# A block kernel's last product: from eight and eight to ten and ten feature tiles in seven half-size products

## The chip, the cores and the metric

The kernel runs on one core of one Trainium2 chip. The metric is the device time of one execution in microseconds (us). The core has five engines that run side by side, each with its own instruction queue in order: TensorE (PE, matmuls; PEld is its loading of the stationary operand), VectorE (DVE), ScalarE (ACT), GpSimd (POOL) and SyncE (SP). SP and POOL here mostly issue transfers, which 16 DMA engines carry out. A transfer that adds to what lies at its destination is issued by POOL; plain ones go out from SP.

## The reference, cut to what matters

The program is one layer of an encoder on 512 tokens (T) of width 1024 (D): a first feed-forward half-step, a mixer, a second feed-forward half-step (FFN2) and a final norm. The change touches the end of FFN2 and the final norm:

```python
D_FF = 2816
x = x + 0.5 * swiglu(rms_norm(x, ffn2_norm), ffn2_w1, ffn2_w3, ffn2_w2)
out = rms_norm(x, final_norm)

def swiglu(h, w1, w3, w2):
    return (jax.nn.silu(h @ w1) * (h @ w3)) @ w2
```

The last product is `H @ w2`, with `H` of 512 tokens by 2816 features and `w2` of 2816 by 1024. In tiles of 128 that is four token tiles, 22 feature tiles and two column halves of 512. All is float32; each operand is cut into a high part (`hi`, in a reduced format of TensorE) and the rest (`lo`), and three matmuls (hi hi, lo hi, hi lo) make one product.

## The kernel before, in words

**Seven products for eight.** `ByTokens.run` makes the last product with tokens as rows. Of the 22 feature tiles, the first `KS` = 8 (half 1) and the next 8 (half 2) go through the scheme in which a product of two matrices, each cut into two by two blocks, takes seven block products and some sums instead of eight products. The blocks of `H` are token halves by feature halves, those of `w2` feature halves by column halves. The products are called M1 to M7. The remaining 6 feature tiles (`plain`, from `KP` = 16 on) are multiplied in the plain way, first for two banks ("F"), later for the two others ("L").

**Units.** Work is cut into units of two feature tiles. Each unit of a product is 12 matmuls of 128 rows by 512 columns. `order` lists the units: M1, M2, F, M5, M6, M3, M7, L for column half 1, M4, L for column half 0. The loop at the end runs over `n`: `product(n)` issues the matmuls of unit n, then the steps of `plan[n]` are issued, then `ready(n + 3)` prepares the unit three ahead. The last three units are multiplied by `final`, first for token tile 2, then for the two halves of token tile 3. Nearly every instruction is issued under `keep`, so that each engine executes in the order that the code gives.

**Preparation.** `prep` casts a weight tile of 128 x 1024 to its high part on ScalarE (line 1979) and makes the rest on VectorE (line 1905), in one of three pairs of buffers; so a cast waits until TensorE is done with the unit three back. For M6, M3 and M7 `parts` also cuts a sum of blocks of `H` (`S2`, `S4`, `S3`).

**Sums of H.** For each unit u, `wa` and `wb` put the high and low parts of the two halves together (`R[u]`), `s1` to `s4` make the four sums, and `cast` and `rest` write the cut first sum over the second half of the tokens of `h` (units of M5 read it from there).

**Sums of w2.** They are made by transfers: `chain[u]` is loaded with block 11, and adding transfers from POOL (`onto`, line 1896) then put further blocks on it, each when `ready` is done with the state before: block 12 after M1, block 22 after M5, block 21 after M3 (for M4). `b21` and `b22` hold blocks 21 and 22; after M3, block 12 is added onto `b22` (for M7). Plain loads go through `fetch` (line 1892) from SP.

**Results.** Banks X, Y, Z, W hold the sums on TensorE's side. `first_snap`, `fifth_snap` and `sixth_snap` (line 2007) scale what stands in X, Z and X again into SBUF tiles `x0`, `m5` and `up`. `c11`, `c22`, `c12` add or subtract banks (line 1908). `residual` adds the layer's input from a DRAM copy (`xtok`) by transfers from POOL. `square_of`, `measure`, `finish` and `others` do the final norm for token tiles 0 and 1 and prepare that of 2 and 3: squares with their sum on ScalarE (line 2100), the root by a logarithm and an exponential (lines 2108, 2109), scaling and storing.

Of the kernel before, what the change touches and what calls it, by code (L numbers as in the profile page):

```python
# [13 lines left out]
ALU = mybir.AluOpType  # L14
# [7 lines left out]
KD = D // P  # L22
DFF = 2816
KF = DFF // P
KS = 8
DA = 512
NP = DA // P
C = 32
# [24 lines left out]
def kernel(  # L53
# [335 lines left out]
    def f32(ap):  # L389
        return ap.bitcast(F32)  # L390
# [1461 lines left out]
    class ByTokens:  # L1852
# [27 lines left out]
        def run(s, hh, hl, h, w2, hp):  # L1880
# [3 lines left out]
            def part(k0, c):  # L1884
                return w2[0][k0 * P:(k0 + 2) * P, c * T:(c + 1) * T].rearrange("(k p) c -> p k c", p=P)
# [4 lines left out]
            def fetch(tag, k0, c):  # L1890
                to = unit(tag)
                keep(nc.sync.dma_start(to, part(k0, c)))
                return to

            def onto(to, src):
                keep(nc.gpsimd.dma_start(to, src, accum_op=ALU.add))
# [7 lines left out]
            def two(to, a, b, op=ALU.subtract):  # L1904
                keep(dve.tensor_tensor(to, a, b, op=op))

            def three(to, ps, f, b, op=ALU.add):
                keep(dve.scalar_tensor_tensor(to, ps, f, b, op0=ALU.mult, op1=op))

            chain = [t[:] for t in s.sv.first_raw]  # L1910
            for u in (2, 3):
                chain.append(wp.tile([P, 2, T], F32, tag="raw", name="raw", bufs=4)[:])
                keep(nc.sync.dma_start(chain[u], part(2 * u, 0)))
            X, Y = [bank(f"tx{a}", pr) for a in range(2)], [bank("ty0", pr), bank("ty1")]
            Z, W = [bank("tz0"), bank("tz1", pf)], [bank(f"tw{a}", pf) for a in range(2)]
            bank_of = [[Y[0], Z[0]], [Y[1], Z[1]], [X[0], W[0]], [X[1], W[1]]]

            def single(tag, name):
                return xp.tile([P, 2, H], F32, name=name, tag=tag)[:]

            S2, S4 = [fp.tile([P, 8, H], F32, name=f"s{i}", tag=f"O{i}") for i in range(2)]
            S2, S4 = [[S[:, 2 * u:2 * u + 2] for u in range(NU)] for S in (S2, S4)]
            S3 = [xp.tile([P, 2, H], F32, name="s3", tag="acc", bufs=2)[:] for _ in range(2)]
            S3 += [fp.tile([P, 2, H], F32, name="s3", tag="sq7")[:], single("rstd", "s3")]
            R = [None] * NU

            def wa(u):
# [4 lines left out]
            def wb(u):  # L1932
                for k in range(2):
                    kk = KS + 2 * u + k
                    to = R[u][1][k]
                    two(over(to, hh[kk]), f32(hh[kk]), f32(hl[kk]), ALU.add)

            def s1(u):
                v = R[u][1][2][:, :, H:T]
                two(v, R[u][0][2][:, :, H:T], v)  # L1940

            def cast(u):
                keep(act.copy(h[:, 2 * u:2 * u + 2, 0, H:T], R[u][1][2][:, :, H:T]))

            def rest(u):
                hi, lo = [h[:, 2 * u:2 * u + 2, i, H:T] for i in range(2)]
                two(lo, R[u][1][2][:, :, H:T], f32(hi))

            def s2(u):
                two(S2[u], R[u][1][2][:, :, H:T], R[u][0][2][:, :, 0:H])  # L1950

            def s3(u):
                two(S3[u], R[u][0][2][:, :, 0:H], R[u][0][2][:, :, H:T])

            def s4(u):
                two(S4[u], R[u][1][2][:, :, 0:H], S2[u], ALU.add)
# [17 lines left out]
            def prep(src):  # L1974
                if len(wide) % 3 == 2:
                    hi, lo = fp.tile([P, 2, T], F32R, name="whi", tag="fg")[:], unit("E30", F32R, "wlo")
                else:
                    hi, lo = [wp.tile([P, 2, T], F32R, tag=t, name=t, bufs=2)[:] for t in ("whi", "wlo")]
                keep(act.copy(hi, src))
                two(lo, src, f32(hi))  # L1980
                wide.append((hi, lo))

            def seventh(n, banks, left, start=False):
# [25 lines left out]
                return got  # L2009

            K2, KP = KS, 2 * KS
            b21 = [fetch(t, K2 + 2 * u, 0) for u, t in enumerate(("E10", "E11", "E20", "E21"))]
            plain = range(KP, KF, 2)

            def all_of(m):
                return [(m, u) for u in range(NU)]

            order = all_of("M1") + all_of("M2") + [(("F", k0), c) for k0 in plain for c in range(2)]
            order += all_of("M5") + all_of("M6") + all_of("M3") + all_of("M7") + [(("L", k0), 1) for k0 in plain]
            order += all_of("M4") + [(("L", k0), 0) for k0 in plain]  # L2020
            made = {}

            def source(m, u):
                if m in ("M1", "M5", "M6", "M4"):
# [7 lines left out]
            def ready(n):  # L2032
                m, u = order[n]
                if m in ("M6", "M3", "M7"):
                    made["left", m, u] = parts({"M6": S2, "M3": S4, "M7": S3}[m][u])
                if n > 1:
                    prep(source(m, u))
                if m == "M1":
                    onto(chain[u], part(2 * u, 1))
                if m == "M5":  # L2040
                    onto(chain[u], part(K2 + 2 * u, 1))
                if m == "M3":
                    onto(made["b22", u], part(2 * u, 1))
                    if u == NU - 1:
                        for v in range(NU):
                            onto(chain[v], part(K2 + 2 * v, 0))

            def product(n):
                m, u = order[n]
# [27 lines left out]
                made["m5"] = snap(Z, "m5", 2)  # L2077

            def sixth_snap():
                made["up"] = snap(X, "up", 0)  # L2080

            def c11():
                for a in range(2):
# [5 lines left out]

            def c12():  # L2090
                for a in range(2):
                    three(made["up"][a], Z[a][:], sc[:, a:a + 1], made["up"][a], ALU.subtract)

            def residual(name, t0, c):
                for a in range(2):
# [7 lines left out]
            def biased(t, q):  # L2103
                keep(dve.tensor_scalar(sc[:, 16 + t:17 + t], q, 1.0 / D, RMS_EPS, op0=ALU.mult, op1=ALU.add))
# [4 lines left out]
                keep(act.activation(r, r, AF.Exp, scale=-0.5))  # L2109

            def gains():
                made["fg"] = hp.tile([P, D], F32, name="fgain", tag="E01")[:]
# [5 lines left out]

            def square_of(name, t):
                biased(t, square(made[name][t], t, 0))  # L2120

            def measure(t):
                root(t, square(made["up"][t], t, 1))
# [2 lines left out]
                keep(nc.sync.dma_start(out[0, t * P:(t + 1) * P, c * T:(c + 1) * T], src))  # L2126

            def finish(t):
                for c, src in ((0, made["x0"][t]), (1, made["up"][t])):
                    three(src, src, sc[:, 20 + t:21 + t], made["fg"][:, c * T:(c + 1) * T], ALU.mult)  # L2130
                    store(t, c, src)

            def others():
                for a in range(2):
# [9 lines left out]
                3: [lambda: rest(0), lambda: wa(1), lambda: load("F", 16, 0, "E10")],  # L2144
                4: [lambda: wb(1), lambda: load("F", 16, 1, "E11")],
                5: [first_snap, lambda: s1(1), lambda: s2(1), lambda: load("F", 18, 0, "E20")],
                6: [lambda: cast(1), lambda: s3(1), lambda: s4(1), lambda: load("F", 18, 1, "E21")],
                7: [lambda: rest(1), lambda: wa(2)],
                8: [lambda: wb(2), lambda: load("F", 20, 0, "E10")],
                9: [lambda: s1(2), lambda: s2(2), lambda: load("F", 20, 1, "E11")],  # L2150
                10: [lambda: cast(2), lambda: s3(2), lambda: s4(2)],
                11: [lambda: rest(2), lambda: wa(3), lambda: b22(0, "E20")],
                12: [lambda: wb(3), lambda: b22(1, "E21")],
                13: [lambda: s1(3)],
                14: [lambda: cast(3), lambda: s2(3)],
                15: [lambda: rest(3), lambda: s4(3)],
                16: [lambda: s3(3)],
                17: [fifth_snap],
                18: [lambda: b22(2, "E00"), lambda: b22(3, "E01")],
                21: [sixth_snap, lambda: load("L", 16, 1, "E10")],  # L2160
                22: [c11, lambda: load("L", 18, 1, "E11")],
                24: [lambda: c22(W, sc), lambda: residual("x0", 0, 0)],
                25: [lambda: load("L", 20, 1, "E20")],
                27: [act_set, lambda: load("L", 16, 0, "E21")],
                28: [lambda: load("L", 18, 0, "E00"), gains],
                29: [lambda: load("L", 20, 0, "E10")],
                30: [lambda: c22(X, neg)],
                31: [lambda: residual("m5", 2, 1), kept],
                33: [c12, lambda: residual("up", 0, 1)],
                34: [lambda: square_of("x0", 0), lambda: square_of("x0", 1)],  # L2170
                36: [others],
            }
            for n in range(-1, len(order) - 3):
                if n >= 0:
# [84 lines left out]
```

## Time and profile before

| | |
|---|---|
| median of 3 runs | 1118.36 us (1118.07 to 1118.51) |
| the profiled execution's own time | 1118.83 us |
| its span, first to last instruction | 1117.1 us |
| granted TensorE clock | 0.999 |
| TensorE busy | 99% of the span |
| the last product, first to last matmul | 1002.12 to 1111.19 us |

The span is that of the program's instructions in one profiled execution; what lies around it, 1.73 us, belongs to the measured time. In rows of the timeline a number in brackets is the time that the engine stood idle before the instruction, followed by what ended it. A group's mean duration can be longer than the step from one start to the next, since an engine begins an instruction before the one ahead of it has wholly ended.

### The profile page before, as it was taken

The page shows a single profiled execution, that of the slowest core. Times are in us where ns is not written, and L with a number is a line of the kernel's source. Part 1 is how long each engine was busy: PE and PEld are TensorE (multiplying, and loading weights), DVE is VectorE, ACT ScalarE, POOL GpSimd, SP SyncE. Part 2 cuts the span into 40 slices and gives each one's busy share as a digit, 9 for nine tenths or more (in the row PEclk, how much of TensorE's full clock was granted, in tenths as well). Part 3 has the DMA queues.
Part 4 walks back from the last instruction along what each step waited for, and adds up shares of the span by engine and source line. Part 5 has one row for each costly group of instructions (what it writes and reads, how often), then busy time and mean ns, then how long its engine had stood idle before and what let it go on. Part 6 is the DMA issues. An engine that isn't in the chain of part 4 may idle for free.

```text
span 1117.1 us, 19566 instructions
## 1 busy us (share of the span) xinstructions
PE 1109.1 (99%) x7658; PEld 975.8 (87%) x7658; DVE 910.8 (82%) x1427; ACT 651.2 (58%) x1088; POOL 110.9 (10%) x175
## 2 busy tenths in 40 slices
PE   9999999999999999999999999999999999999997
PEld 7899999998887888888777787788999999998886
DVE  6889999989556788768777677878889999989876
ACT  6646555644335855454779768534766655655564
POOL 2000000010000112321000001113000000001240
PEclk9999999999999999999999999999999999999999
DMA  8433333353344343345322226543344433358696
GB/s 265 128 94 105 114 96 112 96 180 110 116 123 119 83 118 102 113 121 140 78 58 74 86 89 199 163 132 95 97 121 123 132 96 114 96 168 226 152 213 184
DMA packets 199322, 140.60 MB, mean 126 GB/s; under 512 B 10654, under 2 KB 178910, under 8 KB 199230
## 3 DMA queue, kind: packets, MB, share of 16 engines
q1 hardware_dynamic: 186094, 110.51, 33.8%
q0 software_dynamic: 10752, 27.79, 10.1%
q8 instruction: 60, 0.98, 0.4%
q10 hardware_dynamic: 2384, 1.05, 0.3%
q14 instruction: 32, 0.26, 0.1%
HBM read 124.45 MB, written 14.88 MB: 125 GB/s over the span
## 4 chain that ended last, share of the span: by engine, by line
PE 97%; DVE 1%; DMA 1%; ACT 0%; issue 0%; SPq 0%; DVEq 0%
PE za L143 23%; PE zc L143 14%; PE pgt L143 8%; PE pd L143 6%; PE pk L143 6%; PE tx L1902 4%; PE ppj L1702 4%; PE pw L143 4%; PE pq L143 4%; PE pb L143 3%; PE pa L143 3%; PE tz L1902 3%; PE pv L143 2%; PE ty L1902 2%; PE pl L143 1%; PE lp L1490 1%
## 5 line engine op out<-in xcount | busy, mean ns | idle before, releaser
L134 ACT CAST whi<-raw 128x1024 fp32r<-128x1024 f32 (+2 forms) x93 | 90.0, 969 | 101.8 <-issue 16.6
L135 DVE TENSOR_TENSOR wlo<-raw,whi 128x1024 fp32r<-128x1024 f32 (+2 forms) x93 | 104.5, 1123 | 21.3 <-ACT whi L134 20.9
L143 PE MATMUL zc<-xh,wlo 128*128 128x256 f32 x296 | 83.7, 283 | 0.0
L143 PE MATMUL zc<-xl,whi 128*128 128x256 f32 x296 | 83.7, 283 | 0.0
L143 PE MATMUL zc<-xh,whi 128*128 128x256 f32 x296 | 83.7, 283 | 0.0
L143 PE MATMUL za<-e,wtwo 128*128 128x256 f32 x480 | 64.2, 283 | 0.0
L143 PEld LDWEIGHTS za<-e,wtwo 128*128 128x128 f32 x480 | 59.6, 188 | 0.0
L512 ACT CAST wtwo<-wsum 128x1024 fp32r<-128x1024 f32 x37 | 38.9, 1051 | 31.4 <-PE za L143 31.4
L143 PEld LDWEIGHTS zc<-xl,whi 128*128 128x128 f32 x296 | 56.7, 191 | 0.0
L143 PEld LDWEIGHTS zc<-xh,wlo 128*128 128x128 f32 x296 | 56.7, 191 | 0.0
L143 PEld LDWEIGHTS zc<-xh,whi 128*128 128x128 f32 x296 | 56.6, 191 | 0.0
L143 PE MATMUL pgt<-xh,whi 128*128 128x512 f32 x128 | 53.0, 414 | 0.0
L515 DVE TENSOR_TENSOR wlo<-raw,whi 128x1024 fp32r<-128x1024 f32 x41 | 50.0, 1219 | 2.5 <-ACT whi L512 2.5
L524 DVE TENSOR_TENSOR wsum<-wsum,raw 128x512 f32<-128x512 f32 x74 | 50.9, 688 | 1.2
L524 DVE TENSOR_TENSOR wsum<-raw 128x512 f32<-128x512 f32 x74 | 50.7, 685 | 0.0
L143 PE MATMUL pgt<-xh,wlo 128*128 128x512 f32 x128 | 50.1, 391 | 0.0
L143 PE MATMUL pgt<-xl,whi 128*128 128x512 f32 x128 | 50.0, 391 | 0.0
L512 ACT CAST whi<-wsum 128x1024 fp32r<-128x1024 f32 x37 | 38.8, 1048 | 16.9 <-PE zc L143 13.0
L512 ACT CAST whi<-raw 128x1024 fp32r<-128x1024 f32 x41 | 43.1, 1051 | 8.9 <-PE zc L143 7.9
L598 ACT ACTIVATE fs<-fa 128x512 f32<-128x512 f32 x39 | 24.7, 632 | 38.5 <-DVE fa L631 31.3
L515 DVE TENSOR_TENSOR wtwo<-wsum,wtwo 128x1024 fp32r<-128x1024 f32 x37 | 45.1, 1218 | 0.0
L515 DVE TENSOR_TENSOR wlo<-wsum,whi 128x1024 fp32r<-128x1024 f32 x37 | 45.1, 1218 | 0.0
(692 smaller groups left out, 3619.2 us busy)
## 6 DMA issues: line engine op xcount, KB each, us to landing
raw<-in_ffn_w_dram SPq DMA_DIRECT2D x106, 512.0 KB
raw<-in_w_in_dram SPq DMA_DIRECT2D x40, 512.0 KB
wu<-in_ffn_w_dram SPq DMA_DIRECT2D x20, 512.0 KB
raw<-in_ffn_w_dram POOLq DMA_DIRECT2D x12, 512.0 KB, 7.6
raw<-in_w_out_dram SPq DMA_DIRECT2D x8, 512.0 KB
raw<-in_ffn_w_dram SPq DMA_DIRECT2D x8, 384.0 KB
gsave<-gs SPq DMA_DIRECT2D x9, 256.0 KB
xin<-in_x_dram SPq DMA_DIRECT2D x4, 512.0 KB
```

The costliest lines, as they stand in the source:

```text
L134: marks["wide"] = act.copy(hi[:], raw[:])
L135: marks["rest"] = (eng or dve).tensor_tensor(lo[:], raw[:], hi[:].bitcast(F32), op=ALU.subtract)
L143: mm = pe.matmul(ps, w, x_, start=first and n == 0, stop=last and n == 2, skip_group_check=chain)
L512: keep(act.copy(dst, src))
L515: keep(dve.tensor_tensor(dst, src, f32(hi), op=ALU.subtract))
L524: keep(dve.tensor_tensor(to, a, b, op=ALU.add))
L598: keep(act.activation(sa[:], a_[:], AF.Silu))
L1490: keep(pe.matmul(av[half(q), j * P:(j + 1) * P], vt[k][:, h * 64:(h + 1) * 64], s.trs[q][:, o:o + P], start=k == 0, stop=k == b))
L1702: keep(pe.matmul(ps[:], a[:, k, :], y[k][b], start=k == 0 and n == 0, stop=k == NP - 1 and n == 2))
L1902: keep(pe.matmul(ps[:], a, b, start=start, stop=stop, skip_group_check=True))
```

## The change

`KS` goes from 8 to 10: 20 of the 22 feature tiles go through the seven products (five units each), and one unit of two feature tiles stays plain. Because there is no room for all weights, three of them (two of `b21` and one of F) are loaded as two half tiles each into tiles `x5`, `x6` and `x7` that held the norm's input (`halved`, `pair`). The sums of H's high and low parts for the fifth unit are made by transfers within SBUF into `x5` and `x6` (`joined`: two copies from SP and two adding transfers from POOL for each half), and its further sums go tile by tile (`each`). M5 and M6 take the units in the order 0, 1, 2, 4, 3. The adding transfers of M4's first two units are issued after M6 instead of after M3; the residuals of `m5` and `up` earlier. `up` is snapped with a negative factor, so that its residual can be added before `c12`, and `c12` adds. `square_of` also multiplies `x0` by the gain; `measure` and `finish` move from behind the loop to steps 34 and 35, and `finish` scales `x0` on ScalarE instead of VectorE.

```diff
-KS = 8
+KS = 10
...
+            chain.append(fetch("E10", 8, 0))
...
+            def pair(n, name):
+                return [xp.tile([P, T], F32, name=f"{name}{i}", tag=f"x{i}{n}")[:] for i in "hl"]
+
+            def halved(n, k0, c):
+                to = pair(n, "wh")
+                for k in range(2):
+                    keep(nc.sync.dma_start(to[k], w2[0][(k0 + k) * P:(k0 + k + 1) * P, c * T:(c + 1) * T]))
+                return to
+
+            def joined(u, n):
+                if R[u] is None:
+                    R[u] = []
+                R[u].append(pair(5 + n, f"r{n}"))
+                ks = [n * KS + 2 * u + k for k in range(2)]
+                for to, kk in zip(R[u][n], ks):
+                    keep(nc.sync.dma_start(over(to, hh[kk]), f32(hh[kk])))
+                for to, kk in zip(R[u][n], ks):
+                    onto(over(to, hh[kk]), f32(hl[kk]))
+
+            def each(u, to, a, b, op=ALU.subtract):
+
+                if len(R[u][0]) == 3:
+                    two(to[2], a[2], b[2], op)
+                else:
+                    for k in range(2):
+                        two(to[k], a[k], b[k], op)
...
-            b21 = [fetch(t, K2 + 2 * u, 0) for u, t in enumerate(("E10", "E11", "E20", "E21"))]
+            b21 = [fetch(t, K2 + 2 * u, 0) for u, t in enumerate(("E11", "E20", "E21"))]
+            b21 += [halved(7, K2 + 6, 0), halved(5, K2 + 8, 0)]
             plain = range(KP, KF, 2)
+            turns = 0, 1, 2, 4, 3
...
-            made = {}
+            made = {(("F", KP), 0): halved(6, KP, 0)}
...
                     onto(made["b22", u], part(2 * u, 1))
-                    if u == NU - 1:
-                        for v in range(NU):
-                            onto(chain[v], part(K2 + 2 * v, 0))
+                if m == "M3" and u == NU - 1 or m == "M6" and u < 2:
+                    for v in range(2, NU) if m == "M3" else (u,):
+                        onto(chain[v], part(K2 + 2 * v, 0))
...
-                made["up"] = snap(X, "up", 0)
+                made["up"] = snap(X, "up", 24)
...
-                    three(made["up"][a], Z[a][:], sc[:, a:a + 1], made["up"][a], ALU.subtract)
+                    three(made["up"][a], Z[a][:], sc[:, a:a + 1], made["up"][a])
...
             def square_of(name, t):
                 biased(t, square(made[name][t], t, 0))
+                two(made[name][t], made[name][t], made["fg"][:, 0:T], ALU.mult)
...
             def finish(t):
-                for c, src in ((0, made["x0"][t]), (1, made["up"][t])):
-                    three(src, src, sc[:, 20 + t:21 + t], made["fg"][:, c * T:(c + 1) * T], ALU.mult)
-                    store(t, c, src)
+                r, x, up = sc[:, 20 + t:21 + t], made["x0"][t], made["up"][t]
+                keep(act.activation(x, x, AF.Copy, scale=r))
+                store(t, 0, x)
+                three(up, up, r, made["fg"][:, T:D], ALU.mult)
+                store(t, 1, up)
...
+                7: [lambda: rest(1), lambda: wa(2), lambda: joined(4, 0)],
+                8: [lambda: wb(2), lambda: joined(4, 1), lambda: b22(0, "E20")],
+                9: [lambda: s1(2), lambda: s2(2), lambda: b22(1, "E21")],
+                10: [lambda: cast(2), lambda: s3(2), lambda: s4(2)],
+                11: [lambda: rest(2), lambda: wa(3)],
+                12: [lambda: s1(4), lambda: wb(3), lambda: b22(2, "E11")],
+                13: [lambda: cast(4), lambda: s1(3), lambda: rest(4)],
+                14: [lambda: cast(3), lambda: s2(3), lambda: rest(3)],
+                15: [lambda: s2(4)],
+                16: [lambda: s4(4)],
+                17: [lambda: s4(3), fifth_snap],
+                18: [lambda: s3(3), lambda: residual("m5", 2, 1)],
+                19: [lambda: s3(4), lambda: b22(3, "E00"), lambda: b22(4, "E01")],
+                21: [sixth_snap],
+                22: [c11],
+                24: [lambda: c22(W, sc), lambda: residual("x0", 0, 0), lambda: residual("up", 0, 1)],
+                25: [lambda: load("L", KP, 1, "E20")],
+                26: [lambda: load("L", KP, 0, "E21")],
+                28: [act_set, gains],
+                31: [lambda: c22(X, neg), kept],
+                33: [c12],
+                34: [lambda: square_of("x0", 0), lambda: square_of("x0", 1), lambda: measure(0), lambda: measure(1)],
+                35: [others, lambda: finish(0), lambda: finish(1)],
...
-            measure(0)
-            measure(1)
-            finish(0)
-            finish(1)
-            ends = list(enumerate(plain, len(order) - 3))
+            ends = list(enumerate((K2 + 6, K2 + 8, KP), len(order) - 3))
```

More of the change, by code (lines that the diff above doesn't have):

```diff
@@ L1921, in run @@
             S2, S4 = [fp.tile([P, 8, H], F32, name=f"s{i}", tag=f"O{i}") for i in range(2)]
-            S2, S4 = [[S[:, 2 * u:2 * u + 2] for u in range(NU)] for S in (S2, S4)]
+            S2, S4 = [[S[:, 2 * u:2 * u + 2] for u in range(4)] + [tmp("s", [P, 2, H])[:]] for S in (S2, S4)]
             S3 = [xp.tile([P, 2, H], F32, name="s3", tag="acc", bufs=2)[:] for _ in range(2)]
-            S3 += [fp.tile([P, 2, H], F32, name="s3", tag="sq7")[:], single("rstd", "s3")]
+            S3 += [fp.tile([P, 2, H], F32, name="s3", tag="sq7")[:], single("rstd", "s3"), tmp("s3", [P, 2, H])[:]]
             R = [None] * NU
@@ L1938, in s1, with rows, whole3 @@
+            def each(u, to, a, b, op=ALU.subtract):
[4 more added lines that the diff above has]
+                        two(to[k], a[k], b[k], op)
+            def rows(ts, c0):
+                return [t[..., c0:c0 + H] for t in ts]
+            def whole3(t):
+                return [t[:, 0], t[:, 1], t]
             def s1(u):
-                v = R[u][1][2][:, :, H:T]
-                two(v, R[u][0][2][:, :, H:T], v)
+                a21, a22 = rows(R[u][0], H), rows(R[u][1], H)
+                each(u, a22, a21, a22)
@@ L1942, in cast @@
             def cast(u):
-                keep(act.copy(h[:, 2 * u:2 * u + 2, 0, H:T], R[u][1][2][:, :, H:T]))
+                to, v = h[:, 2 * u:2 * u + 2, 0, H:T], rows(R[u][1], H)
+                if len(v) == 3:
+                    keep(act.copy(to, v[2]))
+                else:
+                    for k in range(2):
+                        keep(act.copy(to[:, k], v[k]))
             def rest(u):
                 hi, lo = [h[:, 2 * u:2 * u + 2, i, H:T] for i in range(2)]
-                two(lo, R[u][1][2][:, :, H:T], f32(hi))
+                each(u, whole3(lo), rows(R[u][1], H), whole3(f32(hi)))
@@ L1949, in s2 @@
             def s2(u):
-                two(S2[u], R[u][1][2][:, :, H:T], R[u][0][2][:, :, 0:H])
+                each(u, whole3(S2[u]), rows(R[u][1], H), rows(R[u][0], 0))
             def s3(u):
-                two(S3[u], R[u][0][2][:, :, 0:H], R[u][0][2][:, :, H:T])
+                each(u, whole3(S3[u]), rows(R[u][0], 0), rows(R[u][0], H))
             def s4(u):
-                two(S4[u], R[u][1][2][:, :, 0:H], S2[u], ALU.add)
+                each(u, whole3(S4[u]), rows(R[u][1], 0), whole3(S2[u]), ALU.add)
@@ L1978, in prep @@
                     hi, lo = [wp.tile([P, 2, T], F32R, tag=t, name=t, bufs=2)[:] for t in ("whi", "wlo")]
-                keep(act.copy(hi, src))
-                two(lo, src, f32(hi))
+                if type(src) is list:
+                    for k in range(2):
+                        keep(act.copy(hi[:, k], src[k]))
+                    for k in range(2):
+                        two(lo[:, k], src[k], f32(hi[:, k]))
+                else:
+                    keep(act.copy(hi, src))
+                    two(lo, src, f32(hi))
                 wide.append((hi, lo))
@@ L2011, in run, with all_of @@
             K2, KP = KS, 2 * KS
-            b21 = [fetch(t, K2 + 2 * u, 0) for u, t in enumerate(("E10", "E11", "E20", "E21"))]
+            b21 = [fetch(t, K2 + 2 * u, 0) for u, t in enumerate(("E11", "E20", "E21"))]
+            b21 += [halved(7, K2 + 6, 0), halved(5, K2 + 8, 0)]
             plain = range(KP, KF, 2)
-            def all_of(m):
-                return [(m, u) for u in range(NU)]
+            turns = 0, 1, 2, 4, 3
+            def all_of(m, us=range(NU)):
+                return [(m, u) for u in us]
             order = all_of("M1") + all_of("M2") + [(("F", k0), c) for k0 in plain for c in range(2)]
-            order += all_of("M5") + all_of("M6") + all_of("M3") + all_of("M7") + [(("L", k0), 1) for k0 in plain]
+            order += all_of("M5", turns) + all_of("M6", turns) + all_of("M3") + all_of("M7") + [(("L", k0), 1) for k0 in plain]
             order += all_of("M4") + [(("L", k0), 0) for k0 in plain]
-            made = {}
+            made = {(("F", KP), 0): halved(6, KP, 0)}
             def source(m, u):
@@ L2111, in gains @@
             def gains():
-                made["fg"] = hp.tile([P, D], F32, name="fgain", tag="E01")[:]
+                made["fg"] = hp.tile([P, D], F32, name="fgain", tag="E11")[:]
                 keep(nc.sync.dma_start(made["fg"], final_norm.unsqueeze(0).broadcast_to([P, D])))
@@ L2143, in run @@
                 2: [lambda: cast(0), lambda: s3(0), lambda: s4(0)],
[L2144 to L2149, printed above, removed]
@@ L2150, in run @@
-                9: [lambda: s1(2), lambda: s2(2), lambda: load("F", 20, 1, "E11")],
-                10: [lambda: cast(2), lambda: s3(2), lambda: s4(2)],
[L2152 to L2171, printed above, removed]
+                3: [lambda: rest(0), lambda: wa(1), lambda: load("F", KP, 1, "E11")],
+                4: [lambda: wb(1)],
+                5: [first_snap, lambda: s1(1), lambda: s2(1)],
+                6: [lambda: cast(1), lambda: s3(1), lambda: s4(1)],
```

## The prediction

> **What bounds the kernel now.** I read the page first: its span, its busy table and the chain that ended last.
>
> ```profile
> span 1117.1 us, 19566 instructions
> PE 1109.1 (99%) x7658; PEld 975.8 (87%) x7658; DVE 910.8 (82%) x1427; ACT 651.2 (58%) x1088; POOL 110.9 (10%) x175
> PE 97%; DVE 1%; DMA 1%; ACT 0%; issue 0%; SPq 0%; DVEq 0%
> ```
>
> TensorE sets the end. Then I read the chain in order of time over the last product (columns: start, us, what, count).
>
> ```profile
> 1002.12 10.91 PE tx L1902 x48
> 1013.03 13.60 PE ty L1902 x60
> ...
> 1091.91 14.96 PE tx L1902 x66
> 1106.87 2.15 PE tz L1902 x18
> 1109.02 2.17 PE tx L1902 x18
> ...
> 1111.22 0.49 DVE yt L1908
> ...
> 1113.33 0.40 DVEq L2255
> ```
>
> The stage runs from 1002.12 to 1111.19 without a gap. A unit (two feature tiles, twelve 512-wide matmuls) takes 13.60 / 5 = 2.72 us, and 40 units at 2.72 are 108.8 of the 109.07 us. The last three units are cut differently: token tile 2 first, 18 matmuls that end at 1106.87, then tile 3 in two halves, 2.15 + 2.17 us. After the last matmul a tail of 5.9 us goes to the span's end. So what TensorE does less is gained, provided that no weight or left operand comes late. What stands behind TensorE is read from the timelines of VectorE and ScalarE around 1027 to 1042 (start, duration, instruction).
>
> ```profile
> 1026.85 1.22 DVE L1905 TENSOR_TENSOR wlo<-wu,whi 128x1024 fp32r<-128x1024 f32 x1
> ...
> 1036.87 1.22 DVE L1905 TENSOR_TENSOR wlo<-raw,whi 128x1024 fp32r<-128x1024 f32 x1
> 1038.01 1.29 DVE L1905 TENSOR_TENSOR rb<-hh,hl 128x512 f32<-128x512 f32 x2
> ...
> 1040.35 0.68 DVE L1905 TENSOR_TENSOR rb<-ra,rb 128x512 f32<-128x512 f32 x1
> 1040.95 1.22 DVE L1905 TENSOR_TENSOR wlo<-raw,whi 128x1024 fp32r<-128x1024 f32 x1
> ```
> ```profile
> 1036.64 1.06 ACT L1979 CAST whi<-raw 128x1024 fp32r<-128x1024 f32 x1 [1.62 <-PE ty L1902]
> ```
>
> VectorE runs back to back; from start to start a full weight rest costs 1.14 us, a 512-wide add 0.6. ScalarE casts the weight three units ahead, as soon as TensorE releases the buffer.
>
> **The change, part by part.** *Products.* Seven products of 4 units and 12 plain units (40) become seven of 5 and 4 plain (39): one unit of 2.72 us goes. With every other time kept, TensorE would end at 1108.47 and token tile 2 at 1104.15.
>
> *Feature tiles 8, 9, 18, 19.* Their sum of high and low parts is made by eight 256 KB transfers inside SBUF (four copies from SP, four adding ones from POOL) instead of VectorE. They start when the weights that lie in the same tiles have been cut up: the second pair follows the rest of unit 10, 1026.85 + 1.14 = 1028.0 (one step more or less from the halved form is below 0.1). VectorE needs them in `s1(4)`, behind the rest of unit 14, 1036.87 + 1.14 = 1038.0. No transfer of this kind is in the trace. The nearest rows are the transfer rates (stretch, busy of PE, PEld, DVE, ACT, POOL, clock, DMA share, GB/s): weight loads alone, adding transfers alone, both together, stores of 256 KB.
>
> ```profile
> 1052.00:1056.00 4.00, 4.00 (x20) 3.30 (x19) 3.02 (x4) 3.22 (x5) 0.00 (x0) 1.00 1.05 402
> 1042.00:1050.00 8.00, 8.00 (x37) 6.64 (x36) 7.36 (x10) 4.20 (x5) 2.57 (x3) 1.00 1.12 197
> 1078.00:1096.00 18.00, 18.00 (x81) 14.92 (x80) 11.60 (x13) 8.51 (x10) 3.24 (x4) 1.00 1.10 266
> ...
> 1106.00:1108.00 2.00, 2.00 (x15) 1.85 (x14) 2.00 (x4) 0.31 (x1) 0.00 (x0) 1.00 1.01 381
> ```
> ```profile
> wu<-in_ffn_w_dram POOLq DMA_DIRECT2D x4, 512.0 KB, 5.7
> ```
>
> An adding transfer of 0.524 MB moves in 0.524 / 0.197 = 2.7 us, so 3.0 of the 5.7 us to landing are fixed. Low end: copies at 381 GB/s (0.7 each) with 1 us fixed land at 1030.4, and the two adding ones at 1030.4 + 3.0 + 2 x 1.33 = 1036.1. High end: the copies take the 3.0 too and the adding ones share the engines with the loads of `b22` issued just behind (266 / 2 = 133 GB/s, 1.97 each): 1032.4 + 3.0 + 3.9 = 1039.3. I take 1038, nearer the high end since those loads are certain. After it VectorE has `s1(4)` 0.7, `wb(3)` 1.2, a rest 1.14, `s1(3)` 0.7, `rest(4)` 0.7: 4.4 us, so 1042.4, and unit 15 (the fifth product's unit 4) starts at 1002.12 + 15 x 2.72 = 1042.9. Cost 0, with 0.5 us to spare; at the high end 0.8 us. Queued behind `s1(4)` on VectorE are the rests of units 15 to 17, for which TensorE waits two units later.
>
> *VectorE's other work*: the fifth unit's five combinations are 3.3 us against one rest less (1.14) and no `wa`, `wb`; from step 12 to 19 each step has 2.3 to 3.0 us of work in 2.72. Hidden by the two units that weights are ahead; without that cover 1 us.
>
> *Loads and freed tiles.* `chain[4]` and five `b21` go out at once, three in tiles freed with the last slots before 1002; 512 KB at 402 GB/s is 1.3 us. Beside the adding transfers these loads take 3.9 us each at worst, and the last is wanted at unit 7's end, 1023.9; from 1001, six at half rate are in by 1024.6 at the very latest, at full rate by 1009; TensorE wants unit 10 only at 1029.3. Cost 0.
>
> *The queue of adding transfers late in the stage.* Before, POOL issues these (start, us, what):
>
> ```profile
> 1069.13 1.20 POOL L1896 DMA_DIRECT2D wu<-in_ffn_w_dram  x1 [1.72 <-DVE wlo L1905]
> 1069.86 5.34 POOL L1896 DMA_DIRECT2D raw<-in_ffn_w_dram  x4
> 1072.72 4.26 POOL L1896 DMA_DIRECT2D x<-xtok  x2
> 1086.37 1.72 POOL L1896 DMA_DIRECT2D m<-xtok  x2 [9.39 <-PE tz L1902]
> 1094.48 1.73 POOL L1896 DMA_DIRECT2D up<-xtok  x2 [6.39 <-DVE up L1908]
> ```
>
> The landing line of the two `x` transfers says how deep that queue is: they go out from 1072.72 on and land at about 1094.6 and 1096.7, 2.1 us apart, which is the half share of 266.
>
> ```profile
> DMA to landing us min/median/max: 21.9/22.7/23.5
> ```
>
> After the fourth M3 transfer (1069.13 + 5.7 = 1074.8) the changed queue holds one more of M3, three of M4, two `x`, two `up`: 4 x 0.524 + 4 x 0.262 = 3.14 MB. Beside it SP loads two weights, the gains and `yt`, 2.1 MB. Shared: 2 x 2.1 / 0.266 = 15.8 us; the other 1.04 MB alone: 5.3 us. The second `up` lands at about 1074.8 + 21.1 + 0.6 = 1096.5. Bounds: 1094 if the loads take little of it, 1099 if the queue starts one unit later.
>
> *The end.* Here I expect the gain to go. `c12` used to run before its residual was added; now it reads it, so VectorE waits there for `up` (before: 1093.27), with the rests of units 36 to 38 behind it. And `measure` and `finish` stand ahead of the casts of units 37 and 38, where before they followed all casts. Rows of ScalarE and VectorE:
>
> ```profile
> 1093.76 1.06 ACT L1979 CAST whi<-raw 128x1024 fp32r<-128x1024 f32 x1 [1.67 <-PE tx L1902]
> 1094.71 0.63 ACT L2100 ACTIVATE junk<-x 128x512 f32<-128x512 f32 x1
> ...
> 1100.15 0.63 ACT L2100 ACTIVATE junk<-m 128x512 f32<-128x512 f32 x1
> ...
> 1100.78 0.62 ACT L2100 ACTIVATE junk<-m 128x512 f32<-128x512 f32 x1
> ...
> 1102.88 0.62 ACT L2100 ACTIVATE junk<-up 128x512 f32<-128x512 f32 x1
> ...
> 1104.06 0.62 ACT L2100 ACTIVATE junk<-up 128x512 f32<-128x512 f32 x1
> ```
> ```profile
> 1061.80 1.27 ACT L2007 ACTIVATE up<-tx,small 128x512 f32<-128x512 f32 x2 [0.92 <-PE tx L1902]
> ```
> ```profile
> 1092.13 1.23 DVE L1905 TENSOR_TENSOR wlo<-raw,whi 128x1024 fp32r<-128x1024 f32 x1 [1.49 <-ACT whi L1979]
> 1093.27 1.40 DVE L1908 SCALAR_TENSOR_TENSOR up<-tz,small,up 128x512 f32<-128x512 f32 x2
> ...
> 1101.49 0.68 DVE L1905 TENSOR_TENSOR m<-m,fgain 128x512 f32<-128x512 f32 x1
> ...
> 1104.19 0.75 DVE L1908 SCALAR_TENSOR_TENSOR x<-x,small,fgain 128x512 f32<-128x512 f32 x1
> 1104.86 0.74 DVE L1908 SCALAR_TENSOR_TENSOR up<-up,small,fgain 128x512 f32<-128x512 f32 x1
> ...
> 1106.91 1.14 DVE L1908 SCALAR_TENSOR_TENSOR yt<-tx,small,yt 128x512 f32<-128x512 f32 x2
> ```
>
> From start to start: a cast 0.95, a square 0.63, a `measure` 1.18, a ScalarE scaling 0.64, a VectorE 512-wide step 0.6 to 0.7. With `up` landing at L: second `c12` L + 0.1 to L + 0.8; rest 36 to L + 1.9; the small sum that the root waits for, L + 2.1; first root L + 2.6; second `measure` L + 3.8; cast 37 L + 4.8; two squares of `m` L + 6.0; two scalings L + 7.3; cast 38 L + 8.3. VectorE: rest 37 to L + 6.0, two products with the gain L + 7.3, two of `up` L + 8.6, rest 38 L + 9.9. Token tile 2 needs unit 38's low part for its last two matmuls, 0.45 us: it ends at L + 10.35, and TensorE at L + 10.35 + 4.32 = L + 14.7. With L = 1096.5 that is 1106.85 and 1111.2, against 1106.87 and 1111.19 before: 2.7 us of waiting on the path, as much as was saved. The tail behind is the same.
>
> *Sum*: -2.72 (a unit) + 2.7 (units 37 and 38) + 0 to 0.3 (unit 15, half weighed) = about +0.1 us. The profiled execution took 1118.83 us, 1.73 beyond its span, 0.47 above the median 1118.36; on the median this gives 1118.5.
>
> **The rivals.** *(a) Nearly the whole gain.* L is early, 1094 or less. ScalarE's own order then decides: cast 36 ends at 1094.7, four squares and two roots to 1098.3, cast 37 1099.3, squares and scalings 1101.8, cast 38 1102.8, where TensorE wants it at 1102.76; rest 38 comes 0.6 late. Time 1118.36 - 2.72 + 0.6 = 1116.2, or 1115.6 if that vanishes too. For it: the two early M4 transfers and `m` leave this queue. Against it: 266 GB/s is measured just there. [...]
>
> *(b) Slower: the added sums block VectorE.* If the SBUF transfers land after 1038.5, TensorE waits at unit 15 for the excess, and all later transfers, which are issued in step with the units, move with it, L too. Each us late costs one: a landing at 1041.5 (two loads of `b22` ahead of the adding ones, 3.9 each instead of shared) gives +3.0 + 0.1, 1121.5. It is slower than before from about 1038.5 and by 0.2% from 1040.7. For it: VectorE's 13 us without a gap; against: the high end above is 1039.3.
>
> *(c) The late queue is longer than I count*, L = 1099: +2.5, 1120.9.
>
> **How the numbers follow.** Forecast (1117 to 1120) 0.50; (a) 0.22; (b) 0.14; (c) 0.14. A difference under 0.2% (2.2 us) can't be told from none. Of (a) most, and little else, is beyond it: faster 0.20. Of (b) and (c) nearly all, slower 0.27; same 0.53. The range reaches from (a) with its 0.6 us nearly gone, 1115.8, to (c), 1121.0; the forecast's own is 1117 to 1120.
>
> **What would show it.** Twelve matmuls fewer in the stage; a gap on TensorE before the units 37 and 38 of token tile 2, between 1101 and 1106, released by ScalarE or VectorE; VectorE idle at `c12` for the landing of `up` at 1095 to 1098. No gap there and an end at 1108.5 would prove the forecast wrong, and (a) right; a gap at 1043 would show (b).

## The result and the profile after

The kernel after takes 1124.49 us (median; 1123.60 to 1125.31) against 1118.48 (1118.07 to 1118.94) for the one before on the same chip: ratio 1.0053, 95% interval 1.0038 to 1.0069. It is slower by 6.0 us. A fifth execution of the kernel after took 1199.69 us at a granted clock of 0.85, which is a slower state of the chip and is not counted. The forecast was 1118.5 with a range to 1121.0, so the time lies outside the range, on the side of rival (b).

The profiled execution took 1125.31 us, the longest of the four. From its page: span, busy table and the chain by engine.

```profile
span 1123.6 us, 19600 instructions
PE 1110.7 (99%) x7646; PEld 976.4 (87%) x7646; DVE 915.1 (81%) x1442; ACT 653.4 (58%) x1097; POOL 119.5 (11%) x183
PE 93%; DVE 4%; DMA 1%; issue 1%; ACT 1%; DVEq 0%; POOLq 0%; ACTq 0%
```

There are 12 matmuls fewer (7646 for 7658), one unit as planned, and yet TensorE is busy 1.6 us longer. TensorE's share of the chain fell from 97% to 93%: other engines now set part of the end. The waits of TensorE (what, released by, us in total, times, longest) name three in this stage, where before had none:

```profile
PE tz L1902 <- DVE h L1905: 2.9, 1, 2.9
PE tx L1902 <- ACT whi L2024: 1.4, 1, 1.4
PE tx L1902 <- DVE wlo L1905: 0.5, 1, 0.5
```

The first is at unit 15, the place of rival (b). The timeline of TensorE there, then the windows (stretch, length, busy time of PE, PEld, DVE, ACT, POOL, granted clock, DMA share, GB/s):

```profile
1042.43 0.39 PE L1902 MATMUL tz<-whi,h 128*128 128x512 f32 x1
1045.76 3.35 PE L1902 MATMUL tz<-whi,h 128*128 128x512 f32 x7 [2.94 <-DVE h L1905]
```
```profile
1042.00:1044.00 2.00, 0.82 (x4) 0.36 (x2) 1.99 (x4) 1.35 (x2) 0.00 (x0) 1.00 1.11 202
1044.00:1046.00 2.00, 0.24 (x1) 0.24 (x2) 2.00 (x5) 0.59 (x2) 0.93 (x1) 0.72 1.14 208
1046.00:1048.00 2.00, 2.00 (x5) 1.58 (x6) 2.00 (x4) 2.00 (x4) 0.80 (x2) 0.50 1.12 203
1048.00:1052.00 4.00, 4.00 (x11) 3.12 (x10) 4.00 (x7) 1.58 (x3) 1.85 (x2) 0.54 1.13 204
1052.00:1060.00 8.00, 8.00 (x36) 6.58 (x36) 5.86 (x9) 4.21 (x6) 2.93 (x3) 1.00 1.08 189
```

Two losses lie here, one behind the other. TensorE stands for 2.94 us, which makes its work 3.1 us late (3.33 us from one start to the next instead of 0.23). Then it works at half its clock: seven matmuls take 3.35 us, and 2 us at 0.50, 4 us at 0.54 and 0.24 us at 0.72 leave undone 1.00 + 1.84 + 0.07 = 2.9 us of work. "Busy" hides that loss; only the clock column shows it. The size of the second loss belongs to this execution, whose mean clock is 0.995: the three others have 0.997, 0.997 and 0.999 and took 1124.49, 1124.39 and 1123.60 us. The last section comes back to this.

What TensorE waited for stands in VectorE's timeline, and behind that in POOL's and SP's:

```profile
1038.81 0.42 DVE L1905 TENSOR_TENSOR r1h<-r0h,r1h 128x256 f32<-128x256 f32 x1 [0.88 <-DMA r1h<-hl]
1042.01 0.43 DVE L1905 TENSOR_TENSOR r1l<-r0l,r1l 128x256 f32<-128x256 f32 x1 [2.77 <-DMA r1l<-xl]
...
1045.63 0.42 DVE L1905 TENSOR_TENSOR h<-r1l,h 128x256 fp32r<-128x256 f32 x1
```
```profile
1027.43 0.89 POOL L1896 DMA_DIRECT2D r0h<-h  x1 [13.46 <-DVE wlo L1905]
1028.45 0.85 POOL L1896 DMA_DIRECT2D r0l<-h  x1
1030.24 0.84 POOL L1896 DMA_DIRECT2D r1h<-hl  x1 [0.94 <-DMA r1h<-hh]
1033.60 1.19 POOL L1896 DMA_DIRECT2D r1l<-xl  x1 [2.53 <-DVE s L1905]
```
```profile
1027.94 0.65 SPq L1954 DMA_DIRECT2D r1l<-xh  x1
1028.64 2.61 SPq L1892 DMA_DIRECT2D wu<-in_ffn_w_dram  x3
```

VectorE stands for `r1l` until 1042.01, with `wb(3)` and the rests behind it. The chain of waits names the same two transfers, the copy and the adding one on it:

```profile
1027.94 5.09 DMA r1l<-xh
1033.60 8.31 DMA r1l<-xl
1045.76 8.28 PE tz L1902 x23
```

The copy, issued just ahead of three loads of `b22`, takes 5.09 us; the adding transfer lands at 1033.60 + 8.31 = 1041.91. `r1h` had landed about 3.1 us earlier.

The second place is the end. There the waits show VectorE's `c12`, then TensorE's token tile 2:

```profile
1100.96 0.75 DVE L1908 SCALAR_TENSOR_TENSOR up<-tz,small,up 128x512 f32<-128x512 f32 x1 [1.95 <-DMA up<-xtok]
1102.40 0.75 DVE L1908 SCALAR_TENSOR_TENSOR up<-tz,small,up 128x512 f32<-128x512 f32 x1 [0.69 <-DMA up<-xtok]
```
```profile
1110.54 0.50 PE L1902 MATMUL tx<-whi,xh 128*128 128x512 f32 x1 [1.40 <-ACT whi L2024]
...
1112.19 0.50 PE L1902 MATMUL tx<-wlo,xh 128*128 128x512 f32 x1 [0.45 <-DVE wlo L1905]
```

`up` landed at 1102.38, 5.9 us later than forecast, and the casts and rests of the last units wait behind what hangs on it. With two short stretches of 0.33 us each at 1107.14 and 1108.40 the steps here are 3.1 us too long.

The sum for the profiled execution: the stage starts about 0.33 us earlier (first matmul 1001.61 for 1001.96), a unit goes (2.72), the stand at unit 15 costs 3.1, the low clock 2.9, the end 3.1: -0.33 - 2.72 + 3.1 + 2.9 + 3.1 = +6.05. The last matmul ends at 1117.25 for 1111.19, which is +6.06. The tail behind it is 0.4 us longer, 6.3 us for 5.9, and with it the sum is the whole difference of the two spans (1123.6 for 1117.1).

### The profile page after: what moved, and what is told of

It is laid out like the page before. It is cut to its first block, busy times and chain, and to the rows that moved or that the text cites. A ratio compares the mean times of both kernels' runs of the same rounds, so it can differ in the third digit from the quotient of the medians.

```text
span 1123.6 us, 19600 instructions
## 1 busy us (share of the span) xinstructions
PE 1110.7 (99%) x7646; PEld 976.4 (87%) x7646; DVE 915.1 (81%) x1442; ACT 653.4 (58%) x1097; POOL 119.5 (11%) x183
## 4 chain that ended last, share of the span: by engine, by line
PE 93%; DVE 4%; DMA 1%; issue 1%; ACT 1%; DVEq 0%; POOLq 0%; ACTq 0%
PE za L143 23%; PE zc L143 14%; PE pgt L143 8%; PE pd L143 6%; PE pk L143 6%; PE ppj L1702 4%; PE pw L143 4%; PE pq L143 4%; PE tx L1902 3%; PE pa L143 3%; PE pb L143 3%; PE tz L1902 2%; PE pv L143 2%; DVE wlo L1905 1%; PE pl L143 1%
```

## The experiments

All start from the kernel after. Ratios are to the kernel before, run beside them: 1118.42 us for the runs with copies only, the tail back, zero matmuls and the loads later, 1118.68 for the four others. "Theory" is: late sums within SBUF at unit 15, with a fall of the clock after the stand, and an end tied to the landing of `up`. The rival readings were that one of the two places explains the other, or that the fall of the clock is a cause of its own.

**Copies only.** The four adding transfers of `joined` go, so the fifth unit's sums hold the high parts of features 8, 9, 18 and 19 alone. The copies and everything that waits for them stay.

```diff
-                for to, kk in zip(R[u][n], ks):
-                    onto(over(to, hh[kk]), f32(hl[kk]))
```

> The four adding transfers within SBUF for feature tiles 8, 9, 18, 19 are left out (the fifth unit's sums are made from the high parts alone). Theory (the late sums block VectorE, TensorE waits at unit 15 and then runs at a lowered clock): the copies land by about 1033, no wait at unit 15, the clock stays at 1.00, the last 'up' residual lands near 1096.5, and only the wait at the end stays (2.7 us): about 1118.5 us. Rival (the stage is held up by the transfers as a whole, whichever they are): the wait moves to another unit and the time stays above 1122.

Measured: 1119.61 us (ratio 1.0014, 1.0005 to 1.0024), ten executions from 1118.96 to 1121.91; the median is 1.1 over the 1118.5 expected. The profiled one took 1119.36. Its windows around unit 15, its `c12` and its waits in this stage:

```profile
1044.00:1046.00 2.00, 2.00 (x10) 1.65 (x10) 2.00 (x3) 1.72 (x3) 0.88 (x1) 1.00 1.13 204
1046.00:1048.00 2.00, 2.00 (x11) 1.65 (x10) 2.00 (x5) 0.90 (x2) 1.18 (x1) 1.00 1.10 194
```
```profile
1096.51 0.75 DVE L1908 SCALAR_TENSOR_TENSOR up<-tz,small,up 128x512 f32<-128x512 f32 x1 [0.77 <-DMA up<-xtok]
```
```profile
PE tx L1902 <- ACT whi L2022: 1.4, 1, 1.4
...
PE tx L1902 <- DVE wlo L1905: 0.5, 1, 0.5
```

Without the adding transfers there is no stand and no fall of the clock, and the rest goes nearly as the prediction said: `up` lands at 1096.48 (forecast 1096.5), the end is 3.2 us longer than undisturbed steps would make it, the last matmul ends at 1111.33 (forecast 1111.2). The tail of 6.3 us is longer here too. So the adding transfers cost 4.9 us in the median (1124.49 - 1119.61). They do not explain the end: that wait is there without them.

**The tail back behind the loop.** `measure` and `finish` for token tiles 0 and 1 again follow all casts.

```diff
-                34: [..., lambda: measure(0), lambda: measure(1)],
-                35: [others, lambda: finish(0), lambda: finish(1)],
+                34: [lambda: square_of("x0", 0), lambda: square_of("x0", 1)],
+                35: [others],
...
+            measure(0)
+            measure(1)
+            finish(0)
+            finish(1)
```

> Measure and finish are issued behind the loop again, everything else as in the changed kernel. Theory (ScalarE's order holds back the casts of units 37 and 38): the wait at unit 15 and the low clock stay (6 us), the wait in token tile 2 at the end (3.1 us) goes: about 1121.4 us. Rival (VectorE waiting for the late residual in c12 is enough to hold units 36 to 38): the end keeps at least 2 us of waiting, 1123.4 or more.

Measured: 1121.40 us (ratio 1.0024, 1.0015 to 1.0034), 3.1 us less than after. Unit 15 still stands and the clock still falls, the end waits for nothing although `up` lands at 1100.7:

```profile
PE tz L1902 <- DVE h L1905: 2.7, 1, 2.7
```
```profile
1046.00:1048.00 2.00, 2.00 (x7) 1.57 (x6) 2.00 (x4) 1.97 (x4) 1.05 (x1) 0.66 1.13 205
1048.00:1052.00 4.00, 4.00 (x15) 3.16 (x14) 4.00 (x7) 1.59 (x3) 1.32 (x2) 0.75 1.10 200
1100.00:1108.00 8.00, 8.00 (x36) 6.40 (x35) 7.31 (x14) 6.82 (x17) 0.00 (x0) 1.00 0.02 4
```

The low clock lasts 3.4 us in this profile, where it lasted 6.8 in that of after. It is the place of `measure` and `finish`, ahead of the last two casts on ScalarE and the last two rests on VectorE, that ties the end to `up`; the run moves both and does not say which of them, or which of the two queues, counts. An `up` that lands at 1100.7 alone delays no matmul.

**Zero matmuls in the stand.** Fourteen matmuls with a zero stationary operand, 3.3 us, run before unit 15. They add zero to bank X; the operand `zeror` is made once at the start of the kernel. The stand is filled, the data comes as late as before.

```diff
...
+                if n == 15:
+                    for _ in range(14):
+                        mm(X[0], zeror[:], h[:, 0, 0])
```

> 14 matmuls with a zero stationary operand (14 x 0.227 = 3.2 us) are put ahead of unit 15, so that TensorE works on nothing while it would stand still. Theory (the granted clock falls because TensorE stood still): unit 15 goes on at the same moment, 1045.7, but units 15 and 16 run at 1.00 instead of about 0.5: 2.9 us less, about 1121.6 us. Rival (the clock falls in this place for another reason): the clock is again near 0.5 for about 6 us after 1046 and the time stays at 1124.5 or is up to 0.3 longer.

Measured: 1124.66 us (ratio 1.0056, 1.0041 to 1.0071): in time a miss, in mechanism not. The windows at unit 15 and at the end, and the waits of token tile 2 (lines are two higher here):

```profile
1044.00:1046.00 2.00, 2.00 (x10) 1.64 (x9) 2.00 (x5) 1.01 (x2) 1.20 (x1) 1.00 1.12 205
1046.00:1048.00 2.00, 2.00 (x10) 1.62 (x10) 2.00 (x4) 1.91 (x4) 0.94 (x1) 1.00 1.13 206
...
1108.00:1116.00 8.00, 6.69 (x36) 5.98 (x37) 5.14 (x8) 2.54 (x7) 0.00 (x0) 0.79 0.41 156
```
```profile
1105.46 0.50 PE L1904 MATMUL tx<-whi,hh 128*128 128x512 f32 x1 [1.18 <-ACT whi L2026]
1108.86 0.50 PE L1904 MATMUL tx<-whi,xh 128*128 128x512 f32 x1 [1.40 <-ACT whi L2026]
1110.51 0.79 PE L1904 MATMUL tx<-wlo,xh 128*128 128x512 f32 x1 [0.45 <-DVE wlo L1907]
```

With TensorE kept busy the clock stays at 1.00 at unit 15: the fall belongs to the stand, not to the transfers or the time of the stage. But the 2.9 us were given back. The end hangs on `up`, which landed at 1100.70, only 1.7 us earlier than in after; so TensorE, earlier by more than that, stood longer at the end (the gap of 1.18 us, which after does not have), and there the clock fell (0.79 over 8 us, some 1.5 us). The second `up` transfer was issued 2.8 us earlier than in after (1078.2 for 1081.0), but took 22.5 us to land instead of 21.4; why it took longer stays open.

**Loads of `b22` later in the code.** Meant to free the DMA engines for the adding transfers.

```diff
-                8: [lambda: wb(2), lambda: joined(4, 1), lambda: b22(0, "E20")],
-                9: [lambda: s1(2), lambda: s2(2), lambda: b22(1, "E21")],
+                8: [lambda: wb(2), lambda: joined(4, 1)],
+                9: [lambda: s1(2), lambda: s2(2)],
...
+                12: [..., lambda: b22(0, "E20")],
+                13: [..., lambda: b22(1, "E21")],
+                14: [..., lambda: b22(2, "E11")],
```

> The three b22 loads (512 KB each) that run beside the sums are issued at steps 12 to 14 instead of 8, 9 and 12. Theory (the adding transfers within SBUF are late because loads share the DMA engines with them): the last sum lands near 1038 instead of 1041.9, the wait at unit 15 is under 0.6 us, the clock stays up: about 1118.5 to 1119.5 us. Rival (an adding transfer whose source lies in SBUF is slow by itself): the last sum lands at 1041 or later and the time stays at 1123.5 or more.

Measured: 1125.20 us (ratio 1.0064, 1.0048 to 1.0081). It tells nothing of the loads, because they did not move; SP's timeline:

```profile
1028.67 2.60 SPq L1892 DMA_DIRECT2D wu<-in_ffn_w_dram  x3
```

They left at 1028.67 instead of 1028.64: a later step in the code only changed the order on SP's queue, nothing stood between there, and SP issued them right behind the copy of `r1l`. So this run nearly repeats after. TensorE stood 3.16 us at unit 15, more than in after, but the clock was at 0.50 for 3.4 us only.

**Loads of `b22` earlier.** Two of the three go ahead of the copies.

```diff
-                6: [lambda: cast(1), lambda: s3(1), lambda: s4(1)],
+                6: [..., lambda: b22(0, "E20"), lambda: b22(1, "E21")],
...
-                8: [lambda: wb(2), lambda: joined(4, 1), lambda: b22(0, "E20")],
-                9: [lambda: s1(2), lambda: s2(2), lambda: b22(1, "E21")],
+                8: [lambda: wb(2), lambda: joined(4, 1)],
+                9: [lambda: s1(2), lambda: s2(2)],
```

> The loads b22(0) and b22(1) are issued ahead of the fifth unit's transfers on SP (their issue there is tied to free tiles, not to steps, so they go out near 1018 and 1020); b22(2) stays behind. Theory (the adding transfers within SBUF are late because 1.5 MB of loads share the engines with them): two thirds of the loads are out of the way, the last sum lands at 1037.5 to 1039.5, the wait at unit 15 is under 1 us, 1118.5 to 1120.5 us. Rival (they are slow by themselves): the last sum lands at 1041 or later, 1123.5 or more.

Measured: 1121.25 us (ratio 1.0023, 1.0014 to 1.0032). POOL's first adding transfer and VectorE's two sums:

```profile
1030.62 0.89 POOL L1896 DMA_DIRECT2D r0h<-h  x1 [16.22 <-DMA r0h<-h]
```
```profile
1038.61 0.43 DVE L1905 TENSOR_TENSOR r1h<-r0h,r1h 128x256 f32<-128x256 f32 x1 [0.25 <-DMA r1h<-hl]
1040.69 0.43 DVE L1905 TENSOR_TENSOR r1l<-r0l,r1l 128x256 f32<-128x256 f32 x1 [1.66 <-DMA r1l<-xl]
```

With fewer loads beside them the four landings lie 1.3, 1.3 and 2.0 us apart (in after 3.6, 2.8 and 3.1), the first being the rate of 197 GB/s that the prediction used. That agrees with the theory that sharing the DMA engines with the loads stretches them. The run does not leave the loads as the only cause: in after the first of the three gaps also fell in the time of the copies, which landed by 1033.0, while here the copies were done before the adding transfers began to land. And the copies now came behind the loads, and POOL started 3.2 us later, so `r1l` gained only 1.3 us (1040.60), outside the 1037.5 to 1039.5 expected; the time is 0.75 us over the upper end, and short of the rival's 1123.5. TensorE stood 1.2 us at unit 15 and the clock did not fall.

**The fifth unit last in M5 and M6.** The units go in the order 0 to 4, and unit 3's steps ahead of unit 4's. The transfers are untouched.

```diff
-            turns = 0, 1, 2, 4, 3
+            turns = range(NU)
...
-                12: [lambda: s1(4), lambda: wb(3), lambda: b22(2, "E11")],
-                13: [lambda: cast(4), lambda: s1(3), lambda: rest(4)],
-                14: [lambda: cast(3), lambda: s2(3), lambda: rest(3)],
+                12: [lambda: wb(3), lambda: b22(2, "E11")],
+                13: [lambda: s1(3), lambda: cast(3), lambda: s2(3), lambda: rest(3)],
+                14: [lambda: s1(4), lambda: cast(4), lambda: rest(4)],
```

> The fifth product takes its units in the order 0 to 4, and on VectorE s1(4) stands behind rest(3), so that the fifth unit's sums, landing at 1041.9, are wanted one unit (2.72 us) later. Theory (VectorE blocked at s1(4) starves unit 15): no wait at units 15 and 16, clock 1.00 there, 'up' lands at about 1096.5 to 1097.5, TensorE ends 14.8 us after it, 1111.3 to 1112.3: 1119 to 1120 us. Rival (the sums are late by so much that the wait only moves to unit 16): over 1 us of waiting at unit 16, 1121 or more.

Measured: 1120.29 us (ratio 1.0015, 1.0006 to 1.0024), ten executions from 1119.12 to 1121.91. VectorE around the sum:

```profile
1042.41 1.23 DVE L1905 TENSOR_TENSOR wlo<-wu,whi 128x1024 fp32r<-128x1024 f32 x1 [0.26 <-ACT whi L2024]
1043.55 0.42 DVE L1905 TENSOR_TENSOR r1h<-r0h,r1h 128x256 f32<-128x256 f32 x1
1043.89 0.42 DVE L1905 TENSOR_TENSOR r1l<-r0l,r1l 128x256 f32<-128x256 f32 x1
```

`r1l` lands as late as ever, at 1041.96, but nobody wants it before 1043.89; no unit of M5 or M6 stands, and the clock holds there. 4.2 us come back (1124.49 - 1120.29); the time is 0.3 us over the upper end expected. This profile is one of the longer executions (1120.75), and its clock is at 0.50 for 3.4 us at the end. The end still waits 3.2 us for `up`, which lands at 1096.37.

**Both.** The fifth unit last, and the tail back behind the loop: the two diffs above together.

> The same, and measure and finish behind the loop as before the change. Theory (two places cost, unit 15 and ScalarE's order at the end, and nothing else): no wait of TensorE in the stage, 39 units at 2.72, an end of the matmuls at about 1108.5 and 1115.7 us, 0.2% less than the kernel before. Rival (c12 waiting for the late 'up' on VectorE still holds units 36 to 38): 1 to 2 us stay, 1117 to 1118.

Measured: 1116.55 us (1116.21 to 1116.78) against 1118.68 for before, ratio 0.9982, 0.9973 to 0.9991. This is faster than both kernels, by 2.1 and 7.9 us. From its page, and all waits of TensorE in the whole span, none of them in the last product:

```profile
span 1114.8 us, 19602 instructions
```
```profile
PE warm L259 <- DVE ones L85: 1.1, 1, 1.1
PE f L310 <- DVE xh L299: 0.8, 1, 0.8
PE f L310 <- DVE xl L295: 0.2, 1, 0.2
```

The 39 units run with one step 0.3 us too long (at 1103.45) and end at 1108.49, where the prediction put an undisturbed end (1108.47). The time is 0.85 us over the expected 1115.7, of which 0.4 is the tail behind the last matmul, 6.3 us instead of 5.9. With the two kernels that undo one part each, the losses nearly add: fifth unit last 4.2 us with the new tail (1124.49 - 1120.29) and 4.85 with the old (1121.40 - 1116.55); the old tail 3.1 and 3.7.

**Copies only, without `up`'s residual.** On top of the first experiment the layer's input is not added to column half 1 of token tiles 0 and 1, so `c12` waits for no transfer.

```diff
-                24: [..., lambda: residual("x0", 0, 0), lambda: residual("up", 0, 1)],
+                24: [..., lambda: residual("x0", 0, 0)],
```

> As with the copies only (the adding transfers within SBUF left out), and the layer's input is not added to 'up' either, so that c12 waits for nothing late. Theory (at the end two things add: the late 'up', about 2 us, and ScalarE's order, about 0.6 us): 1116.2 to 1116.9 us. Rival (ScalarE's order alone makes the 2.7 us): 1118.3 or more.

Measured: 1117.41 us (ratio 0.9989, 0.9980 to 0.9998), 0.5 over the upper end expected. One wait is left, `PE tx` for `wlo`, and in all the end is 1.0 us too long. Of the 3.2 us at the end the late `up` thus makes 2.2, the place of `measure` and `finish` without it 1.0.

## Why the prediction was wrong, point by point

- *One unit of 2.72 us*: right. With both stands gone, the 39 units take 106.79 us (1001.70 to 1108.49) and the 40 of before 109.23 (1001.96 to 1111.19); with the one step of 0.3 us taken off, the difference is 2.7. The first matmul of before starts at 1001.96 in the timeline; the 1002.12 given further up is where the chain's piece begins.
- *VectorE's other work, cost 0*: right. In the run with both changes no unit of M5 or M6 waits.
- *Loads and freed tiles, cost 0*: right. No wait of TensorE or VectorE in after comes from a load of a weight.
- *Feature tiles 8, 9, 18, 19, landing at 1038, cost 0*: this step failed. The last sum landed at 1041.91, beyond the high end of 1039.3. Both of its parts were undersized. The copies were counted as done at 1030.4 to 1032.4 (the 1 us fixed in the earlier of the two was an estimate that no run shows), and the one of `r1l` took 5.09 us, to 1033.0; the adding transfers were taken 1.33 to 1.97 us apart and lay 2.8 to 3.6 apart. The rate of 266 GB/s came from a stretch in which the adding transfers read DRAM, and the prediction gave half of it to them; beside three loads that follow each other closely it did not carry over. The experiment with earlier loads speaks for sharing; the shares of the loads and of the copies, and what is due to source and destination both lying in SBUF, were not separated.
- *Rival (b), one us for each us after 1038.5*: right as a mechanism. 1041.91 gives 3.4 by that rule, the stand was 3.1 (so the point is 1038.8). That it came so near is partly luck: VectorE's work behind the landing took 3.85 us to TensorE's next start, not 4.4, and TensorE wanted the low part at 1042.66, not 1042.9. The price of the rival was still half of the truth in the profiled execution, since the fall of the clock, 2.9 us, was in no step of the prediction. With 1121.5 + 0.4 + 2.9 = 1124.8 the rival would have come near the time, but that 2.9 is not the same in every execution.
- *The late queue, 1096.5*: right where nothing upstream is late, 1096.48 with copies only and 1096.37 with the fifth unit last. In after it moved with units 15 and 16, to 1102.38, as rival (b) said.
- *The end, landing of `up` plus 14.7 us*: right, 14.87 in after and 14.85 with copies only. That the waiting was 3.1 us and not 2.7 comes from the earlier start of the stage. In two profiles, those with zero matmuls and with the fifth unit last, it was 16.3, and there the clock had fallen too (0.79 over 1108 to 1116 us; 0.50 from 1106.72 to 1110.10).
- *Rival (a)*: it did not hold, since `up` was not early. Its own price was low: the place of `measure` and `finish` costs 1.0 us without a late `up`, not 0.6.
- *Rival (c)*: it did not hold either, since the queue took as long as counted wherever it started in time.
- *The tail behind is the same*: wrong by 0.4 us in after, 6.3 for 5.9, and about as much in every run of the changed kernel. From the end of the last matmul to the issue of the last two stores before and after take 2.2 us each (1111.19 to 1113.35, 1117.25 to 1119.40), so the 0.4 us lie behind that issue; their cause stays open.

The forecast of 1118.5 was thus nearly the time of the kernel without the adding transfers (1119.61). The step that failed is the landing of the fifth unit's sums, forecast for 1038 at no cost: it came at 1041.91 and cost 3.1 us of standing. Behind it the fall of the clock was missing altogether, 2.9 us in the profiled execution, and so was the longer tail, 0.4 us.

## What to carry to other kernels

A transfer that replaces an engine's work is to be costed at the rate that it gets beside the loads issued with it (here landings 2.8 to 3.6 us apart, counted as 1.33 to 1.97), and its consumer is better put where a bad estimate costs nothing: moving the fifth unit one place back gave 4.2 us without making any transfer faster. When a saved unit meets an end that is tied to a late transfer, look at what ties it; here the calls of the norm ahead of the last two casts and rests held 3.1 us. A stand of TensorE cost about twice its length in one profile (2.94 us of it were followed by 2.9 us lost to the clock) and less in another (3.16 us by 1.7), so the granted clock is read beside every gap, in more than one execution.

## What the hardware showed that was not expected

*The clock after a stand.* The clock in these traces is 1.00 or 0.50; the figures between come from windows that hold both. Windows cut to the low stretches, in after, with the tail back, with the loads later, and with the fifth unit last (at the end):

```profile
1044.88:1051.70 6.82, 5.94 (x14) 4.68 (x15) 6.82 (x12) 4.17 (x6) 3.58 (x3) 0.50 1.13 204
```
```profile
1046.64:1050.02 3.38, 3.38 (x10) 2.60 (x9) 3.38 (x7) 2.41 (x4) 1.32 (x2) 0.50 1.11 203
```
```profile
1046.24:1049.65 3.41, 3.41 (x9) 2.63 (x9) 3.41 (x6) 2.41 (x5) 1.46 (x2) 0.50 1.13 205
```
```profile
1106.72:1110.10 3.38, 3.38 (x17) 3.33 (x16) 2.13 (x4) 1.22 (x4) 0.00 (x0) 0.50 0.16 64
```

The low clock thus lasted 3.38 to 3.41 us in three of these profiles and 6.82 in the other, and the longest stand at unit 15 (3.16 us, third line) was not the one with the longest low stretch (2.94 us, first line). A stand of 1.19 us there was followed by none, and with matmuls of zeros in the place of the stand the clock stayed at 1.00. The fall did not come at one place in the stand either: in after TensorE stood from 1042.82 to 1045.76, and the clock fell at 1044.88, within the stand and 2.1 us after its start; with the tail back TensorE went on at 1045.23, and the clock fell only at 1046.64. What sets the moment of the fall and the length of the low stretch is not shown.

*Shorter stands at the end.* Stands of 1.4 and 0.45 us, 1.2 us apart, were followed by a lower clock in some executions and not in others: in the profile with the fifth unit last (1120.75 us) the clock fell, in that with copies only (1119.36) it did not, with the same two stands. The executions with copies only lie in two groups, six from 1118.96 to 1119.75 with a mean clock of 0.998 to 0.999, and four from 1121.05 to 1121.91 with 0.997 to 0.998, while the run with both changes, without such stands, keeps its eleven within 0.6 us. Nine executions with the tail back order themselves in the same way: three at 0.999 took 1119.77 to 1120.26 us, three at 0.997 and 0.998 took 1120.70 to 1121.55, three at 0.995 took 1122.12 to 1122.69. No run here sets the time at which such a stand comes, and what decides whether the clock falls after it is not shown.

*Adding transfers within SBUF.* Four of 256 KB, issued within 6.2 us beside three loads of 512 KB, landed 2.8 to 3.6 us apart; with two of those loads moved ahead, 1.3 to 2.0.
